# Row maxima, operand copies and value products of a prompt's attention, issued in another order

## The chip, the cores and the metric

The kernel runs on one core of a Trainium2 chip. The metric is the time on the device, in microseconds (us), of one launch; the lower the better. The core's engines each work through an instruction queue of their own, in order: TensorE (PE, whose weight loads show as PEld), VectorE (DVE), ScalarE (ACT), GpSimd (POOL), and SyncE (SP), which here only issues DMAs.

## The reference

One step of a two-layer model: layer 0 is a state-space mixer, layer 1 a latent attention with 16 heads. A prompt of 1024 tokens and 32 sample tokens go through both. The change lies in layer 1's attention of the prompt alone:

```python
def chunk_causal_attention(q_nope, q_rope, k_nope, k_rope, v, q_pos, k_pos):
    scale = MLA_QK ** -0.5                      # 64 + 32 columns per head
    k_chunk = k_pos // CHUNK                    # CHUNK = 64
    def block(args):
        qn, qr, qp = args
        s = (jnp.einsum('bqhd,bkhd->bhqk', qn, k_nope)
             + jnp.einsum('bqhd,bkd->bhqk', qr, k_rope)).astype(F32) * scale
        mask = k_chunk[None, :] <= (qp // CHUNK)[:, None]
        p = jax.nn.softmax(jnp.where(mask, s, -jnp.inf), axis=-1).astype(v.dtype)
        return jnp.einsum('bhqk,bkhd->bqhd', p, v)
```

All else (projections, norms, the gates, the mixer of layer 0, the output products) is the same in both kernels.

## The kernel before

Everything is computed in fp32, most products as three matmuls of a split operand: a rounded high part `h` and the rest `l = x - h`, summed as h*h + h*l + l*h. `phase_prompt` handles the 16 heads as 8 **pairs** `p`; a pair has two heads `par` = 0 and 1. Pairs alternate between two sets of operand buffers, `i = p % 2`; in the profile and in the orders below the tile of set `i` and head `par` is `qk` + `i` + `par` (`qk01`: set 0, head 1), with four parts `qh`, `kh`, `ql`, `kl`. 64 of the 128 rows of these tiles hold the head's own columns, and the others the rotary part and a few helper rows: a mask, and one row of `ql` that holds the negated row maxima of the scores, which the score product itself then subtracts.

So the steps of a pair are:

- `prep` (one or two pairs ahead): projections `psqk`, norm (`hn`), result in `hx`.
- `fill(p)`: copies of `hx` into `qh`/`kh` (rounded), the rest `hx - h` into `ql`/`kl` (by DVE for head 0, by POOL for head 1: `L_ENG`), and a DMA from POOL's queue for the rotary rows.
- `row_max(i, par)`: for each of 8 blocks of 128 queries one or two matmuls `s` into a PSUM tile (tag `s1`, two buffers, shared with `pm` and `sums`), each reduced by DVE into a column of `mx`; a last reduction (L1260); a transpose of `mx` by PE into `pm` (L1262); a negated copy by ACT into `mr` (L1264); and a DMA from POOL's queue (L1265) that writes `mr` into the row of `ql`.
- `pair(p)`: three **groups** of scores (`GROUPS`). Of each, 4 key blocks by 2 heads: three matmuls into `st` (two PSUM buffers), `exp` by ACT into `pf` (16 buffers). Behind the group stand its value products (`o`, 8 calls), and the sums over keys: additions of the `pf` tiles into `acc`, DVE for head 0 and POOL for head 1 (L1312 to L1318, one `acc` buffer for each head). `rest`, put behind the products of the next group, multiplies `acc` by ones (`sums`), takes the reciprocal as exp(-ln) and scales `o` (L1331).

While pair `p` is computed, `fill(p + 1)`, the row maxima of pair `p + 1` and `prep(p + 2)` run beside it. `spread` sets their order in the program: each stream has a number of steps, a step `k` of `n` stands at (k + 0.5) / n of the pair, and steps are sorted by it. A scheduler then moves instructions on each queue by its own estimate of times; what it made of both programs is shown with the change. Value projections (`psv`) of the next two pairs are put behind the second pair of two.

Of the kernel before, what the change touches and what calls it, by code (L numbers as in the profile page):

```python
# [10 lines left out]
F32 = mybir.dt.float32  # L11
F32R = mybir.dt.float32r
AF = mybir.ActivationFunctionType
ALU = mybir.AluOpType
# [3 lines left out]
P = 128  # L18
# [1097 lines left out]
L_ENG = ("vector", "gpsimd")  # L1116
# [56 lines left out]
def run(*gens):  # L1173
    for g in gens:
        for _ in g:
            pass


LEAD = 0.05


def spread(*streams):

    order = sorted(((k + 0.5) / n - lead, i) for i, (_, n, lead) in enumerate(streams) for k in range(n))
    for _, i in order:
        next(streams[i][0], None)
    run(*(g for g, _, _ in streams))


def phase_prompt(c, st, pr, before):  # L1190
    nc, tc, I, O = c.nc, c.tc, c.I, c.O
    es = ExitStack()
    ap_ = es.enter_context(tc.tile_pool(name="att", bufs=1, reuse_waits="tile"))
    before()
    aq = es.enter_context(tc.tile_pool(name="att2", bufs=1, reuse_waits="tile"))
    krt = ap_.tile([P, 1024], F32, tag="op", name="krt")
    nc.sync.dma_start(krt, c.kr_d[:, :1024])
    bufs = []
# [14 lines left out]
    def fill(p):  # L1213

        i, x = p % 2, pr.x.pop(p)
        qk = bufs[i]
        for par in range(2):
            r, rw = parts(par), rope_rows(par, i)
            eng = L_ENG[par]
            eng = getattr(nc, eng)  # L1220
            for a in range(4):
                dst = qk[("qh", "kh")[a // 2]][par][r, 512 * (a % 2) : 512 * (a % 2) + 512]
                nc.scalar.activation(dst, x[a][r], AF.Copy)
            nc.gpsimd.dma_start(qk["t"][par][rw, 0::2], pr.rope[rw])
            for a in range(4):
                cols = slice(512 * (a % 2), 512 * (a % 2) + 512)
                h, l = qk[("qh", "kh")[a // 2]][par][r, cols], qk[("ql", "kl")[a // 2]][par][r, cols]
                eng.tensor_tensor(l, x[a][r], h.bitcast(F32), op=ALU.subtract)  # L1228

    def values(g):  # L1230
        out = []
# [11 lines left out]
            out.append(vf)  # L1243
        return out

    def row_max(i, par):
        qk = bufs[i]
        qh, ql, kh, kl = (qk[n][par] for n in ("qh", "ql", "kh", "kl"))
        mrow = gap_rows(par, i).start + 10
        mx = ap_.tile([P, 16], F32, tag="mx", name="mx", bufs=2)  # L1250
        for b in range(8):
            n = max(256, 128 * (b + 1))
            ng, w = (1, n) if n <= 512 else (2, n // 2)
            for a in range(ng):
                ps = c.ps.tile([P, 512], F32, tag="s1", name="s1", bufs=2)
                nc.tensor.matmul(ps[:, :w], qh[:, 128 * b : 128 * b + 128], kh[:, a * w : a * w + w], start=True, stop=True)  # L1256
                col = b if b < 4 else 2 * b + a
                nc.vector.tensor_reduce(mx[:, col : col + 1], ps[:, : (w if b else 128)], axis=AX.X, op=ALU.max)  # L1258
            yield
        nc.vector.tensor_reduce(mx[:, 4:8], mx[:, 8:16].rearrange("p (a b) -> p a b", b=2), axis=AX.X, op=ALU.max)  # L1260
        pm = c.ps.tile([P, 512], F32, tag="s1", name="pm", bufs=2)
        nc.tensor.transpose(pm[:8, :128], mx[:, 0:8], c.ident)  # L1262
        mr = ap_.tile([8, 128], F32R, tag="mr", name="mr", bufs=2)
        nc.scalar.activation(mr, pm[:8, :128], AF.Copy, scale=-1.0)  # L1264
        nc.gpsimd.dma_start(ql[mrow : mrow + 1, :], mr)  # L1265

    def pair(p, vt, out):

        i = p % 2
        qk = bufs[i]  # L1270
        for g, (half, pieces) in enumerate(GROUPS):
            pfs = {}
            for j, q0, n in reversed(pieces):
                ks, q = slice(128 * j, 128 * j + 128), slice(q0, q0 + n)
                lo = max(q0, 128 * j) - q0
                for par in range(2):
                    qh, ql, kh, kl = (qk[nm][par] for nm in ("qh", "ql", "kh", "kl"))
                    ps = c.ps.tile([P, 512], F32, tag="st", name="st", bufs=2)
                    for t, (a_, b_) in enumerate(((kh, qh), (kh, ql), (kl, qh))):
                        nc.tensor.matmul(ps[:, :n], a_[:, ks], b_[:, q], start=t == 0, stop=t == 2)  # L1280
                    pf = aq.tile([P, 512], F32, tag="pf", name="pf", bufs=16)
                    nc.scalar.activation(pf[:, lo:n], ps[:, lo:n], AF.Exp, scale=SCALE)
                    f = q0 + lo - 512 * half
                    pfs[j, par] = pf[:, lo:n], slice(f, f + n - lo)
                    yield
            if g < 2:
                po = c.ps.tile([P, 512], F32, tag="o", name="o", bufs=2)

            def product(j, par):
                x, cols = pfs[j, par]  # L1290
                return nc.tensor.matmul(po[parts(par), cols], vt[j][:, i, par], x, start=j == 0,  # L1291
                                        stop=j == 4 * half + 3, skip_group_check=True)

            js = [j for j, _, _ in pieces]
            one = product(js[0], 1)
            with tc.issue_after(one.ins):
                product(js[0], 0)
                for j in js[1:]:
                    for par in range(2):
                        product(j, par)  # L1300
                if left:
                    left.pop()()

            if g < 2:
                acc = [aq.tile([P, 512], F32, tag=f"acc{par}", name="acc") for par in range(2)]
            for par in range(2):
                eng = (nc.vector, nc.gpsimd)[par]
                for k, j in enumerate(js):
                    x, cols = pfs[j, par]
                    a = acc[par][:, cols]  # L1310
                    if g == 2 or k > 1:
                        eng.tensor_tensor(a, a, x, op=ALU.add)  # L1312
                    elif k == 1:
                        f = cols.start
                        x0 = pfs[js[0], par][0]
                        if f:
                            eng.tensor_copy(acc[par][:, :f], x0[:, :f])
                        eng.tensor_tensor(a, x0[:, f:], x, op=ALU.add)  # L1318
            if g != 1:
                def rest(half=half, po=po, acc=acc):  # L1320
                    if half == 0:
                        out["o"] = ap_.tile([P, 1024], F32, tag="op", name="op")
                        out["sg"] = aq.tile([P, 1024], F32, tag="sg", name="sg")
                        nc.sync.dma_start(out["sg"], c.sg_d[p][:, :1024])
                    ps = c.ps.tile([P, 512], F32, tag="s1", name="sums", bufs=2)
                    for par in range(2):
                        nc.tensor.matmul(ps[parts(par)], c.ones[:, :64], acc[par], start=True, stop=True, skip_group_check=True)  # L1327
                    rec = acc[0]
                    nc.scalar.activation(rec, ps, AF.Ln)
                    nc.scalar.activation(rec, rec, AF.Exp, scale=-1.0)  # L1330
                    nc.vector.tensor_tensor(out["o"][:, 512 * half : 512 * half + 512], po, rec, op=ALU.mult)  # L1331
                left.append(rest)

    left = []
    pr.tag = "mm"

    operands(0)
    fill(0)
    run(row_max(0, 0))
    operands(1)  # L1340
    vt = values(0)
    run(row_max(0, 1))
    run(pr.prep(1))
    for p in range(8):
        g, i = p // 2, p % 2
        out = {}
        streams = [(pair(p, vt, out), 24, 0.0)]
        if p < 7:
            fill(p + 1)
            streams.append((itertools.chain(row_max(1 - i, 0), row_max(1 - i, 1)), 16, LEAD))  # L1350
        if p < 6:
            streams.append((itertools.chain(pr.prep(p + 2), pr.rope_block(g + 1) if i == 0 else ()), 6 if i == 0 else 4, LEAD))
# [195 lines left out]
```

## Time and profile before

| | us |
|---|---|
| median of 3 runs | 2036.13 (2035.63 to 2038.16) |
| the profiled execution, its time | 2041.28 |
| the profiled execution, its span (first to last instruction) | 2039.5 |
| of the span: PE busy | 1940.1 (95%) |
| DVE, ACT, POOL busy | 1185.4, 1011.9, 945.5 |
| prompt attention: first `s` matmul to last value product | about 1402 to 1838 |

The profiled execution was 5.2 us longer than the median run. A row of the profile gives the line of the code (a helper's line where a helper records the instruction), the engine, the operation, the tiles as out<-in, the shapes and the count; behind the bar stand busy time, the mean of one instruction in ns, and the engine's idle time just before these instructions with what ended it.

### The profile page before, as it was taken

Reading aid. Unit: us, or ns where it says so; the run is one execution under the profiler, and the core shown is the slowest. Engines: PE = TensorE matmul, PEld = TensorE weight load, DVE = VectorE, ACT = ScalarE, POOL = GpSimd, SP = SyncE. Lnnn points to the kernel's source line nnn. Section 1 sums busy time; section 2 is a strip of 40 time slices with the busy share of each in tenths; the row PEclk is TensorE's granted clock in tenths of the full one; section 3 lists DMA queues with packets and bytes.
Section 4 is the critical chain, followed back from the end, with each engine's and each line's share of the span. In section 5 each row is a group of like instructions: output and inputs, shape, how many; then the busy total and the mean of one; then the engine's idle time right before and its main releaser. Section 6 shows DMA issues by size and latency. Waiting matters only on the chain. (4 is left out here: it accounts for less than half of the span.)

```text
span 2039.5 us, 32319 instructions
## 1 busy us (share of the span) xinstructions
PE 1940.1 (95%) x12787; PEld 1733.4 (85%) x12787; DVE 1185.4 (58%) x1478; ACT 1011.9 (50%) x1875; POOL 945.5 (46%) x771
## 2 busy tenths in 40 slices
PE   8999999999999999999998999998989998889999
PEld 6988899999999998989998999676656565548999
DVE  6888675655757565352475453545465656645544
ACT  4436645455554547242334332875756565543331
POOL 5543534244343454545785441224344443635772
PEclk8999999999999999999999999999989998899999
DMA  4134333424233438453242223436121212315432
GB/s 138 53 84 97 89 94 88 103 74 92 89 77 95 115 80 299 123 181 114 90 127 85 83 95 110 133 92 150 30 59 47 52 40 52 109 53 180 136 122 75
DMA packets 110728, 204.24 MB, mean 100 GB/s; under 512 B 18224, under 2 KB 60720, under 8 KB 110448
## 3 DMA queue, kind: packets, MB, share of 16 engines
q1 hardware_dynamic: 105472, 193.17, 32.3%
q0 software_dynamic: 2800, 6.91, 1.8%
q8 instruction: 100, 1.64, 0.3%
q10 hardware_dynamic: 2304, 2.10, 0.3%
q14 instruction: 52, 0.43, 0.1%
HBM read 156.81 MB, written 38.83 MB: 96 GB/s over the span
## 5 line engine op out<-in xcount | busy, mean ns | idle before, releaser
L205 POOL TENSOR_TENSOR wl<-wraw,wh 128x1024 fp32r<-128x1024 f32 (+2 forms) x185 | 373.1, 2018 | 460.8 <-ACT wh L204 426.2
L215 PE MATMUL mm<-hh,wl 128*128 128x384 f32 (+2 forms) x1152 | 378.0, 328 | 0.0
L215 PE MATMUL mm<-hh,wh 128*128 128x384 f32 (+2 forms) x1152 | 377.1, 328 | 0.8 <-ACT hh L308 0.8
L215 PE MATMUL mm<-hl,wh 128*128 128x384 f32 (+2 forms) x1152 | 375.8, 327 | 0.0
L215 PE MATMUL pso<-yhl,wh 128*128 128x264 f32 x1536 | 285.2, 287 | 3.9 <-DVE yhl L229 1.9
L204 ACT ACTIVATE wh<-wraw 128x1024 fp32r<-128x1024 f32 (+2 forms) x182 | 157.8, 867 | 263.4 <-PE pso L215 102.2
L215 PEld LDWEIGHTS pso<-yhl,wh 128*128 128x128 f32 x1536 | 241.3, 190 | 6.9 <-DVE yhl L229 2.9
L215 PE MATMUL pso<-yhl,wl 128*128 128x264 f32 x768 | 219.9, 287 | 3.0 <-POOL wl L205 3.0
L215 PEld LDWEIGHTS mm<-hh,wh 128*128 128x128 f32 (+1 forms) x1152 | 216.2, 188 | 5.4 <-issue 2.8
L215 PEld LDWEIGHTS mm<-hl,wh 128*128 128x128 f32 (+1 forms) x1152 | 216.6, 188 | 1.6 <-issue 0.7
L215 PEld LDWEIGHTS mm<-hh,wl 128*128 128x128 f32 (+1 forms) x1152 | 216.4, 188 | 1.8 <-issue 0.3
L215 PE MATMUL psi<-yhl,wh 128*128 128x264 f32 (+1 forms) x896 | 166.9, 287 | 3.9 <-ACT yhl L228 3.8
L463 DVE SCALAR_TENSOR_TENSOR cx<-raw,pv,cx 128x1060 f32<-128x1060 f32 x96 | 142.4, 1487 | 41.1 <-ACT cx L461 40.5
L526 ACT ACTIVATE ex<-ex,tokT 128x128 f32<-128x128 f32 (+1 forms) x288 | 87.0, 380 | 133.9 <-DMA ex<-acs_d 126.7
L1258 DVE TENSOR_REDUCE mx<-s 128x1 f32<-128x128 f32 (+2 forms) x192 | 101.7, 552 | 84.5 <-PE s L1256 82.8
L1280 PE MATMUL st<-qk 128*128 128x512 f32 (+2 forms) x576 | 142.9, 378 | 6.8 <-DMA qk<-mr 5.1
L215 PEld LDWEIGHTS pso<-yhl,wl 128*128 128x128 f32 x768 | 146.1, 190 | 3.5 <-POOL wl L205 3.4
L215 PE MATMUL pg<-hH,wl 128*128 128x264 f32 x512 | 145.9, 285 | 0.3 <-POOL wl L205 0.3
L215 PE MATMUL pg<-hH,wh 128*128 128x264 f32 x512 | 145.9, 285 | 0.0
L215 PE MATMUL pg<-hL,wh 128*128 128x264 f32 x512 | 145.7, 285 | 0.0
L215 PEld LDWEIGHTS psi<-yhl,wh 128*128 128x128 f32 (+1 forms) x896 | 138.1, 185 | 5.6 <-ACT yhl L228 4.0
L1280 PEld LDWEIGHTS st<-qk 128*128 128x128 f32 x576 | 105.5, 206 | 35.5 <-issue 9.6
(517 smaller groups left out, 4289.6 us busy)
## 6 DMA issues: line engine op xcount, KB each, us to landing
wraw<-in_inW SPq DMA_DIRECT2D x48, 512.0 KB, 3.5
ex<-acs_d SPq DMA_DIRECT2D x32, 512.0 KB, 5.4
wraw<-in_outW SPq DMA_DIRECT2D x32, 512.0 KB, 3.7
yraw<-y_d SPq DMA_DIRECT2D x32, 264.0 KB, 5.0
u<-u_d SPq DMA_DIRECT2D x32, 264.0 KB, 2.8
eb<-ea_d SPq DMA_DIRECT2D x64, 128.0 KB, 3.9
y_d<-y SPq DMA_DIRECT2D x16, 512.0 KB, 2.9
wraw<-in_gateW SPq DMA_DIRECT2D x16, 512.0 KB, 3.6
```

The lines of the kernel that those rows point to most:

```text
L204: nc.scalar.activation(wh, raw, AF.Copy)
L205: nc.gpsimd.tensor_tensor(wl, raw, wh.bitcast(F32), op=ALU.subtract)
L215: c.nc.tensor.matmul(ps, ww[:, k, :m], aa, start=first and k == 0 and i == 0, stop=last and k == n - 1 and i == 2)
L463: nc.vector.scalar_tensor_tensor(xh, raw[:, k : k + T1], pvc(c, "cw", 4 * b + k), xh, op0=ALU.mult, op1=ALU.add)
L526: nc.scalar.activation(e_, e_, AF.Relu, scale=-1.0, bias=tok(32)[:, i, h : h + 1])
L1258: nc.vector.tensor_reduce(mx[:, col : col + 1], ps[:, : (w if b else 128)], axis=AX.X, op=ALU.max)
L1280: nc.tensor.matmul(ps[:, :n], a_[:, ks], b_[:, q], start=t == 0, stop=t == 2)
```

## The change

Five things are done, all in the prompt's attention:

1. `row_max` no longer ends with the transpose. The transpose, the copy and the DMA (`max_row`) stand behind later scores: those of head 0 behind three steps of head 1's maxima, those of head 1 behind two empty steps.
2. `spread` takes a start and an end for each stream. The maxima run from 0.2 to 0.9 of a pair with 18 steps (before: 16 steps from -0.05 to 0.95), and `fill` becomes a stream of 8 steps from 0 to 0.2 (before: all of it ahead of the pair).
3. In `fill` the rounded copies of head 0 go from ACT to DVE (`tensor_copy`, shown as CAST); those of head 1 stay on ACT. Each copy stands next to its subtraction.
4. The value products, the `acc` additions and the `rest` of a group are issued two key blocks (4 scores) into the next group; those of the last group at the end of the pair as before.
5. The pair's first maxima, ahead of the loop, follow the same scheme.

No matmul, exp, reduction or byte is added or removed; 32 copies change the engine.

```diff
 def spread(*streams):
-    order = sorted(((k + 0.5) / n - lead, i) for i, (_, n, lead) in enumerate(streams) for k in range(n))
+    order = sorted((a + (b - a) * (k + 0.5) / n, i) for i, (_, n, a, b) in enumerate(streams) for k in range(n))
...
     def fill(p):
...
-            for a in range(4):
-                dst = qk[("qh", "kh")[a // 2]][par][r, 512 * (a % 2) : 512 * (a % 2) + 512]
-                nc.scalar.activation(dst, x[a][r], AF.Copy)
             nc.gpsimd.dma_start(qk["t"][par][rw, 0::2], pr.rope[rw])
             for a in range(4):
...
-                eng.tensor_tensor(l, x[a][r], h.bitcast(F32), op=ALU.subtract)
+                if par:
+                    nc.scalar.activation(h, x[a][r], AF.Copy)
+                else:
+                    nc.vector.tensor_copy(h, x[a][r])
+                getattr(nc, L_ENG[par]).tensor_tensor(l, x[a][r], h.bitcast(F32), op=ALU.subtract)
+                yield
...
+    def max_row(i, par, mx):
+        mrow = gap_rows(par, i).start + 10
         pm = c.ps.tile([P, 512], F32, tag="s1", name="pm", bufs=2)
         nc.tensor.transpose(pm[:8, :128], mx[:, 0:8], c.ident)
         mr = ap_.tile([8, 128], F32R, tag="mr", name="mr", bufs=2)
         nc.scalar.activation(mr, pm[:8, :128], AF.Copy, scale=-1.0)
-        nc.gpsimd.dma_start(ql[mrow : mrow + 1, :], mr)
+        nc.gpsimd.dma_start(bufs[i]["ql"][par][mrow : mrow + 1, :], mr)
+
+    def row_maxima(i):
+        mx = [ap_.tile([P, 16], F32, tag="mx", name="mx", bufs=2) for _ in range(2)]
+        yield from row_max(i, 0, mx[0])
+        for k, _ in enumerate(row_max(i, 1, mx[1])):
+            if k == 2:
+                max_row(i, 0, mx[0])
+            yield
+        yield
+        yield
+        max_row(i, 1, mx[1])
...
     def pair(p, vt, out):
...
-            for j, q0, n in reversed(pieces):
+            for k, (j, q0, n) in enumerate(reversed(pieces)):
+                if k == 2 and late:
+                    late.pop()()
...
+            late.append(lambda *a, f=(g, half, [j for j, _, _ in pieces], pfs, po): group(p, vt, out, *f))
+        late.pop()()
...
-        streams = [(pair(p, vt, out), 24, 0.0)]
+        streams = [(pair(p, vt, out), 24, 0.0, 1.0)]
         if p < 7:
-            fill(p + 1)
-            streams.append((itertools.chain(row_max(1 - i, 0), row_max(1 - i, 1)), 16, LEAD))
+            streams.append((fill(p + 1), 8, 0.0, 0.2))
+            streams.append((row_maxima(1 - i), 18, 0.2, 0.9))
```

`group` holds what stood at the end of a group in `pair` before: products, additions, `rest`.

**What the scheduler made of it.** First PE's queue in the middle of pair 1, where the maxima of pair 2's head 0 end. `s` of `qk_14547` are the maxima scores of head 0, `s` of `qk_14548` those of head 1; `st` are pair 1's own scores (x3 is one tile), `pm` the transpose. Before:

```order
L1256 MATMUL s_15480<-qk_14547 128x512
L1280 MATMUL st<-qk_14617 128x512 x3
L1280 MATMUL st<-qk_14616 128x512 x3
L1262 MATMUL pm<-cst,mx 8x128
L1256 MATMUL s_15502<-qk_14548 128x256
L1280 MATMUL st<-qk_14617 128x512 x3
```

And now:

```order
L1251 MATMUL s_15467<-qk_14547 128x512
L1345 MATMUL sums<-acc,ones 64x512 x2
L1293 MATMUL st<-qk_14611 128x512 x3
L1293 MATMUL st<-qk_14612 128x512 x3
L1251 MATMUL s_15503<-qk_14548 128x256
L1251 MATMUL s_15512<-qk_14548 128x256
L1293 MATMUL st<-qk_14611 128x256 x3
L1251 MATMUL s_15521<-qk_14548 128x384
L1293 MATMUL st<-qk_14612 128x256 x3
L1308 MATMUL o<-pf,vf 64x512 x8
L1261 MATMUL pm<-cst,mx 8x128
```

Between the last score of head 0's maxima and the transpose stood two score tiles; now four, the sums, three scores of head 1's maxima and the eight value products.

Second, DVE's queue at the end of pair 1, where the maxima of head 1 end. `mx_15501` (before) and `mx_15370` (after) hold them; the row without `s1` is the last reduction, for which the transpose waits. Before:

```order
L1258 TENSOR_REDUCE mx_15501<-s1_15658 128x1
L1312 TENSOR_TENSOR acc_15579<-acc_15579,pf_15644 128x384
L1312 TENSOR_TENSOR acc_15579<-acc_15579,pf_15609 128x256
L1312 TENSOR_TENSOR acc_15579<-acc_15579,pf_15591 128x128
L1258 TENSOR_REDUCE mx_15501<-s1_15661 128x1
L1260 TENSOR_REDUCE mx_15501<-mx_15501 128x4
```

And now:

```order
L1223 CAST qk10_14611<-hx_15649 64x512
L1223 CAST qk10_14611<-hx_15424 64x512
L1224 TENSOR_TENSOR qk10_14611<-hx_15649,qk10_14611 64x512
L1224 TENSOR_TENSOR qk10_14611<-hx_15424,qk10_14611 64x512
L1253 TENSOR_REDUCE mx_15370<-s1_15577 128x1
L1253 TENSOR_REDUCE mx_15370<-s1_15586 128x1
L1253 TENSOR_REDUCE mx_15370<-s1_15589 128x1
L1253 TENSOR_REDUCE mx_15370<-s1_15598 128x1
L1253 TENSOR_REDUCE mx_15370<-s1_15601 128x1
L1255 TENSOR_REDUCE mx_15370<-mx_15370 128x4
L1349 TENSOR_TENSOR op_15619<-o_15401,acc_15486 128x512
L1334 TENSOR_TENSOR acc_15628<-pf_15519,pf_15500 128x512
```

The three additions that stood ahead of the last maxima have gone behind the last reduction; two of the new casts stand five reductions ahead of it, with their subtractions.

More of the change, by code (lines that the diff above doesn't have):

```diff
@@ L1176, in run @@
             pass
-LEAD = 0.05
 def spread(*streams):
-    order = sorted(((k + 0.5) / n - lead, i) for i, (_, n, lead) in enumerate(streams) for k in range(n))
+    order = sorted((a + (b - a) * (k + 0.5) / n, i) for i, (_, n, a, b) in enumerate(streams) for k in range(n))
     for _, i in order:
         next(streams[i][0], None)
-    run(*(g for g, _, _ in streams))
+    run(*(x[0] for x in streams))
 def phase_prompt(c, st, pr, before):
@@ L1244, in values, with row_max @@
         return out
[L1246 to L1250, printed above, removed]
+    def row_max(i, par, mx):
+        qh, kh = (bufs[i][n][par] for n in ("qh", "kh"))
         for b in range(8):
@@ L1287, in pair @@
                 po = c.ps.tile([P, 512], F32, tag="o", name="o", bufs=2)
-            def product(j, par):
-                x, cols = pfs[j, par]
[L1291 to L1302, printed above, removed]
@@ L1304, in pair @@
-            if g < 2:
-                acc = [aq.tile([P, 512], F32, tag=f"acc{par}", name="acc") for par in range(2)]
-            for par in range(2):
[L1307 to L1332, printed above, removed]
+            late.append(lambda *a, f=(g, half, [j for j, _, _ in pieces], pfs, po): group(p, vt, out, *f))
@@ new lines, in pair, with group, product, rest @@
+        late.pop()()
+    def group(p, vt, out, g, half, js, pfs, po):
+        def product(j, par):
+            x, cols = pfs[j, par]
+            return nc.tensor.matmul(po[parts(par), cols], vt[j][:, p % 2, par], x, start=j == 0,
+                                    stop=j == 4 * half + 3, skip_group_check=True)
+        one = product(js[0], 1)
+        with tc.issue_after(one.ins):
+            product(js[0], 0)
+            for j in js[1:]:
+                for par in range(2):
+                    product(j, par)
+            if left:
+                left.pop()()
+        if g < 2:
+            accs[:] = [aq.tile([P, 512], F32, tag=f"acc{par}", name="acc") for par in range(2)]
+        acc = list(accs)
+        for par in range(2):
+            eng = (nc.vector, nc.gpsimd)[par]
+            for k, j in enumerate(js):
+                x, cols = pfs[j, par]
+                a = acc[par][:, cols]
+                if g == 2 or k > 1:
+                    eng.tensor_tensor(a, a, x, op=ALU.add)
+                elif k == 1:
+                    f = cols.start
+                    x0 = pfs[js[0], par][0]
+                    if f:
+                        eng.tensor_copy(acc[par][:, :f], x0[:, :f])
+                    eng.tensor_tensor(a, x0[:, f:], x, op=ALU.add)
+        if g == 1:
+            return
+        def rest():
+            if half == 0:
+                out["o"] = ap_.tile([P, 1024], F32, tag="op", name="op")
+                out["sg"] = aq.tile([P, 1024], F32, tag="sg", name="sg")
+                nc.sync.dma_start(out["sg"], c.sg_d[p][:, :1024])
+            ps = c.ps.tile([P, 512], F32, tag="s1", name="sums", bufs=2)
+            for par in range(2):
+                nc.tensor.matmul(ps[parts(par)], c.ones[:, :64], acc[par], start=True, stop=True, skip_group_check=True)
+            rec = acc[0]
+            nc.scalar.activation(rec, ps, AF.Ln)
+            nc.scalar.activation(rec, rec, AF.Exp, scale=-1.0)
+            nc.vector.tensor_tensor(out["o"][:, 512 * half : 512 * half + 512], po, rec, op=ALU.mult)
+        left.append(rest)
@@ L1334, in phase_prompt @@
+    late, accs = [], []
     left = []
@@ L1337, in phase_prompt @@
     operands(0)
-    fill(0)
-    run(row_max(0, 0))
+    run(fill(0))
+    ahead = row_maxima(0)
+    for _ in range(8):
+        next(ahead)
     operands(1)
     vt = values(0)
-    run(row_max(0, 1))
+    run(ahead)
     run(pr.prep(1))
@@ L1346, in phase_prompt @@
         out = {}
-        streams = [(pair(p, vt, out), 24, 0.0)]
+        streams = [(pair(p, vt, out), 24, 0.0, 1.0)]
         if p < 7:
-            fill(p + 1)
-            streams.append((itertools.chain(row_max(1 - i, 0), row_max(1 - i, 1)), 16, LEAD))
+            streams.append((fill(p + 1), 8, 0.0, 0.2))
+            streams.append((row_maxima(1 - i), 18, 0.2, 0.9))
         if p < 6:
-            streams.append((itertools.chain(pr.prep(p + 2), pr.rope_block(g + 1) if i == 0 else ()), 6 if i == 0 else 4, LEAD))
+            streams.append((itertools.chain(pr.prep(p + 2), pr.rope_block(g + 1) if i == 0 else ()), 6 if i == 0 else 4, 0.0, 1.0))
         spread(*streams)
```

2 lines of the change are left out of this document (removed).

## The prediction

> **What bounds the kernel now.** I read the page first, for the engine that is full; then the prompt attention's stretch by windows, since the change touches nothing else; then who PE waits for there; then one such wait in order of time.
>
> ```profile
> span 2039.5 us, 32319 instructions
> PE 1940.1 (95%) x12787; PEld 1733.4 (85%) x12787; DVE 1185.4 (58%) x1478; ACT 1011.9 (50%) x1875; POOL 945.5 (46%) x771
> ```
>
> PE is the bound of the whole. The windows give, for each stretch, the busy time of PE, PEld, DVE, ACT and POOL, then the granted PE clock (PEclk), the DMA share and GB/s:
>
> ```profile
> 1402.00:1846.00 444.00, 392.12 (x1805) 261.18 (x1806) 262.87 (x409) 254.03 (x504) 195.03 (x184) 0.94 0.22 59
> 1500.00:1548.00 48.00, 39.79 (x202) 26.90 (x199) 30.78 (x49) 22.14 (x48) 25.19 (x25) 0.89 0.12 34
> 1548.00:1602.00 54.00, 50.48 (x216) 32.87 (x214) 31.44 (x46) 37.97 (x74) 20.25 (x19) 1.00 0.24 66
> 1602.00:1655.00 53.00, 47.03 (x242) 32.11 (x241) 35.55 (x58) 27.78 (x58) 28.49 (x28) 0.94 0.18 44
> 1846.00:2039.00 193.00, 188.96 (x1535) 188.49 (x1534) 95.80 (x92) 61.58 (x86) 112.60 (x60) 1.00 0.43 135
> ```
>
> The first row is the stretch at stake: PE idles 444.0 - 392.1 = 51.9 us, and its clock averages 0.94, so up to 0.06 x 444 = 26.6 us more are lost to slow matmuls. What follows (last row) runs at 98% and full clock. The rows between are single pairs: where PE idles much (8.2 of 48 us) the clock is 0.89, where little (3.5 of 54) it is 1.00. Idling is paid twice. Who PE waits for in that stretch (sum in us, times, longest):
>
> ```profile
> PE pm L1262 <- DVE mx L1260: 18.6, 10, 3.5
> PE s L1256 <- DVE mx L1258: 12.8, 23, 2.0
> PE o L1291 <- ACT pf L1282: 5.4, 11, 0.9
> PE st L1280 <- DMA qk<-mr: 5.1, 2, 2.9
> PE sums L1327 <- DVE acc L1312: 2.9, 1, 2.9
> ```
>
> The largest is the transpose of the maxima, waiting for DVE's last reduction. The rest of the 51.9 us are small waits and gaps without a named cause. One such wait, at the end of pair 0, in order of time (start, duration, engine, line; the last two rows are DVE's last reduction and PE's transpose, with PE's wait in brackets):
>
> ```profile
> 1500.55 0.52 PE L1280 MATMUL st<-qk 128*128 128x256 f32 x3
> 1500.26 3.44 DVE L1312 TENSOR_TENSOR acc<-acc,pf 128x384 f32<-128x384 f32 x3
> 1503.61 0.68 DVE L1258 TENSOR_REDUCE mx<-s 128x1 f32<-128x512 f32 x1
> 1504.33 0.16 DVE L1260 TENSOR_REDUCE mx<-mx 128x4 f32<-128x8 f32 x1
> 1504.54 0.37 PE L1262 MATMUL pm<-cst,mx 128*8 128x128 f32 x1 [3.47 <-DVE mx L1260]
> ```
>
> PE's scores were done at 1501.1. DVE spent 3.44 us on three `acc` additions that nobody was waiting for, and only then did the two reductions (0.84 us). PE's queue is in order, so everything behind the transpose stood still too. DVE isn't short of time: over the stretch it is busy 262.9 of 444 us.
>
> **The change, part by part.**
>
> *Transposes later, additions later (parts 1, 2, 4).* Behind head 0's last `s`, PE now has the sums, four score tiles, three `s` and the eight products before the transpose. Their prices, from another pair:
>
> ```profile
> 1743.81 3.65 PE L1291 MATMUL o<-pf,vf 128*64 128x512 f32 x16
> 1748.31 1.08 PE L1327 MATMUL sums<-acc,ones 128*64 128x512 f32 x4
> 1755.22 0.86 PE L1280 MATMUL st<-qk 128*128 128x512 f32 x3
> ```
>
> 3.65 + 1.08 + two tiles at 0.86 are 6.5 us, and DVE needs 0.84 us of reductions behind the last `s`; even with the 3.44 us of additions ahead of them that is covered. At head 1's end PE's work between last `s` and transpose stays about what it was, but in DVE's queue the three additions have gone behind the reduction: 0.84 us against the sums (1.08) and nine projection matmuls. So these waits should go. I keep one mean wait (18.6 / 10 = 1.9 us) for the step from pair 6 to pair 7, where DVE's new order still mixes seven additions and three splits of the next phase into the maxima, and little else is left to fill PE: **-16.7 us**. Ends: all of it (-18.6), or half (-9.3).
>
> *Copies to DVE (part 3).* Of the 56 copies in the stretch, half move:
>
> ```profile
> L1223 ACT ACTIVATE qk<-hx 64x512 fp32r<-64x512 f32 x56 | 35.0, 625 | 3.0 <-PE st L1280 2.3
> L202 DVE CAST wh<-wraw 128x1024 fp32r<-128x1024 f32 x2 | 1.4, 680 | 0.0
> L1317 DVE COPY acc<-pf x8: 217/852/1542, 1458.3 to 1820.7; 128x128 f32<-128x128 f32 x8
> L1317 POOL COPY acc<-pf x8: 289/290/292, 1462.1 to 1818.8; 128x128 f32<-128x128 f32 x8
> L1258 DVE TENSOR_REDUCE mx<-s 128x1 f32<-128x128 f32 (+2 forms) x192 | 101.7, 552 | 84.5 <-PE s L1256 82.8
> ```
>
> ACT gets back 28 x 0.625 = 17.5 us; it isn't what PE waits for, so I count nothing. The trace has no 64x512 cast on DVE. The nearest row is the 1024-column cast (0.68 us), half of it for 512 columns: 0.34 us alone. But the small COPY on DVE (minimum, median and maximum in ns) ranges from 217 to 1542 while the same copy on POOL stays at 290: DVE copies are held up when POOL works. I take 0.6 us: 28 x 0.6 = 16.8 us more for DVE, which has 181 us idle, 82.8 of them waiting for PE's own `s` (last row). PE pays only where a reduction that it waits for stands behind a cast; I take one in six, +2.8. In turn the additions that stood between reductions are gone from many places; of the 12.8 us of `s` waits I let as much go, -2.8. Together **0**; ends -6.4 (half the `s` waits) and +16.8 (every cast paid by PE).
>
> *Value products two key blocks later (part 4).* `o` won't wait for the exp just ahead of it in groups 0 and 1; at a pair's end nothing changes. Of 5.4 us **-1.5**; ends 0 and -2.7 (half). What it holds longer: 8 + 4 of 16 `pf` buffers, so exps have no new wait; if the additions fell back by a whole group, exps and with them scores would stop.
>
> *Queues and ends.* The first pair's transpose now stands behind three `s` of head 1 and so behind two more reductions (0.55 each, last row above), while the scores that need its row stay where they were: the 5.1 us of waits for `mr` grow by **+1.0** (0 to +2.2). In POOL's queue the `mr` DMA stands among additions as before. SP's output store moves a few places past loads of weights whose wait is not on PE's list: 0. At the very end, `rest` of half 0 comes one score tile later (0.52 us for 256 columns, row at 1500.55), and the chain of additions behind it, for which the sums wait, by as much: **+0.4**.
>
> Idle time: -16.7 + 0 - 1.5 + 1.0 + 0.4 = **-16.8 us**.
>
> *The clock.* In proportion to the idle time that goes: 26.6 x 16.8 / 51.9 = **-8.6 us** (ends: 0, and the whole 26.6).
>
> The Trainium skill (TensorE: Matmul & The Clock Gate, section on HAM oscillation) has the clock fall only after PE idles for more than about 3.4 us. By that rule only waits like the two longest transposes cost clock, both go, and the result would be the rival "clock full" below. The trace doesn't agree: the pair of 1602 to 1655 has a clock of 0.94, and no `s` wait anywhere is longer than 2.0 us.
>
> *What comes back.* PE that no longer waits reaches the next `s` earlier, and there are two PSUM buffers for it; DVE then has 262.9 + 16.8 = 279.7 us of work in some 420, 67% against 59%. I give back **+5 us** (a fifth of 25.4; ends 0 and all).
>
> Sum: -16.8 - 8.6 + 5 = -20.4 us. The profiled execution took 2041.3 us (its span 2039.5 and 1.8 around it), so 2020.9 for it; it was 5.2 us above the median of 2036.1, and from the median I forecast 2015.7, say **2016 us**, own range 2005 to 2026.
>
> **Rivals.**
>
> *The clock stays full.* The idle stretches that are left are too short and too far apart to lower it. For: the pair of 1548 to 1602 idles 3.5 us and has 1.00. Against: the tail's 2.9 us and the wait for `mr` remain. -16.8 - 26.6 + 5 = -38.4: 1998 us. Chance 0.12.
>
> *The wait moves.* DVE is just as late, and PE stops at the next `s` instead. For: `s` waits already happen 23 times. Against: DVE's additions now stand behind the maxima. Half the transposes' gain (-9.3, with -0.1 from the small terms), 4.8 of clock, 5 given back: -9.2, 2027 us. Chance 0.14.
>
> *Nothing comes of it.* PE's waits keep their sum, because DVE and POOL hold each other up, or because the `mr` row, which needs ACT, POOL's issue and the DMA (5.1 us waited for it already, in two waits), lands too late for head 1's scores at each pair's start: 2036 us. Against: DVE's 181 us of idle time. Chance 0.08.
>
> *The casts block DVE (slower).* Each cast waits for the POOL instruction that runs, and the reductions behind it wait too. Place: the four instructions ahead of head 1's last five reductions. At the longest COPY's 1.54 us, all paid by PE, 28 x 1.54 = 43 us: -25.4 + 43 = +17.7, 2054 us. It decides from 25.4 / 28 = 0.9 us per cast paid by PE. For: the COPY's median of 852 against 290. Against: only casts that stand ahead of a reduction due at once count. Chance 0.10.
>
> The Trainium skill (SBUF — State Buffer, section on who interferes with whom) says that VectorE's copies and casts in a two-port mode and GpSimd shut each other out for a whole instruction; the spread of the COPY agrees, and that rule is this rival.
>
> **How the numbers follow.** Forecast 0.56, clock full 0.12, wait moves 0.14, nothing 0.08, casts block 0.10. I predict the likeliest. The range 1997 to 2033 takes in all but the casts, nothing (half of it lies outside), and the far ends of the forecast. A change under 0.2% (4 us) can't be told from none: faster 0.80 (forecast, clock, most of the moved wait), same 0.09, slower 0.11.
>
> **What would show it.** In the profile after: the row of `pm` waiting for `mx` falls from 18.6 to under 4 us; `s` waiting for `mx` stays between 6 and 16; the stretch's PE idle is near 35 us and its clock about 0.96; the CAST's mean is 0.4 to 0.9 us; an undone wait shows as `s` far above 13. If DVE's casts average over 1.2 us, or `st` waits for `mr` at every pair, I am wrong on the sign; if the clock reads 0.99 or more, on the size.

## The result, and the profile after

The changed kernel takes 2051.68 us (median of 4 runs, 2047.70 to 2052.19) against 2036.73 us for the one before: a ratio of 1.0069, 95% interval 1.0051 to 1.0086. It is **slower by 0.7%**, where 2016 us were forecast. The profiled execution has a span of 2050.4 us, 10.9 us more than the one before (which lay 5 us above its median).

The page's first lines, and the attention's stretch by windows, up to the same point of the program (11 us later now):

```profile
span 2050.4 us, 32332 instructions
PE 1943.6 (95%) x12787; PEld 1736.6 (85%) x12787; DVE 1214.5 (59%) x1510; ACT 996.6 (49%) x1843; POOL 953.6 (47%) x771
```

```profile
1402.00:1857.00 455.00, 394.90 (x1807) 264.49 (x1806) 288.89 (x439) 240.89 (x476) 202.42 (x188) 0.92 0.22 59
```

PE idles 455.0 - 394.9 = 60.1 us (before 51.9), its clock is 0.92 (before 0.94), and DVE has 288.9 us of work (before 262.9). Who PE waits for in this stretch, the rows that the prediction has prices for (sum, times, longest):

```profile
PE s L1251 <- DVE mx L1253: 40.7, 22, 5.5
PE st L1293 <- DMA qk<-mr: 4.9, 2, 3.1
PE sums L1345 <- DVE acc L1328: 3.0, 1, 3.0
PE o L1308 <- ACT pf L1295: 2.3, 5, 0.7
```

The transpose's row (`pm`, 18.6 us) is gone, as forecast, and `o` fell from 5.4 to 2.3. But the scores of the maxima, `s`, wait 40.7 us for DVE's reductions instead of 12.8. DVE's groups in the stretch (busy us, mean ns of one, then idle time ahead of them):

```profile
L1253 DVE TENSOR_REDUCE mx<-s 128x1 f32<-128x128 f32 (+2 forms) x192 | 101.7, 551 | 79.5 <-PE s L1251 78.7
L1328 DVE TENSOR_TENSOR acc<-acc,pf 128x256 f32<-128x256 f32 (+1 forms) x64 | 59.5, 930 | 1.4
L1224 DVE TENSOR_TENSOR qk<-hx,qk 64x512 fp32r<-64x512 f32 x28 | 25.4, 918 | 0.2
L1223 DVE CAST qk<-hx 64x512 fp32r<-64x512 f32 x28 | 16.6, 601 | 7.7 <-PE st L1293 7.3
L1349 DVE TENSOR_TENSOR op<-o,acc 128x512 f32<-128x512 f32 x16 | 11.0, 689 | 24.7 <-ACT acc L1348 18.5 <-POOL acc L1334 6.1
```

The rows of the additions and the subtractions before:

```profile
L1312 DVE TENSOR_TENSOR acc<-acc,pf 128x256 f32<-128x256 f32 (+1 forms) x64 | 53.2, 831 | 1.2
L1228 DVE TENSOR_TENSOR qk<-hx,qk 64x512 fp32r<-64x512 f32 x28 | 21.2, 756 | 14.5 <-ACT qk L1223 14.5
```

The reductions take what they took. The additions went from a mean of 831 to 930 ns, the subtractions from 756 to 918, and the casts are new. Among the additions it is the widest that were stretched, the 24 of 128x512 (before, then now):

```profile
L1312 DVE TENSOR_TENSOR acc<-acc,pf 128x512 f32<-128x512 f32 x24 | 22.6, 941 | 0.5
L1328 DVE TENSOR_TENSOR acc<-acc,pf 128x512 f32<-128x512 f32 x24 | 36.3, 1512 | 0.7
```

The longest wait, at the start of pair 1, where the maxima of pair 2 begin, in order of time (DVE, then POOL, then PE):

```profile
1496.25 1.98 DVE L1223 CAST qk<-hx 64x512 fp32r<-64x512 f32 x1 [0.41 <-PE st L1293]
1498.16 0.68 DVE L1334 TENSOR_TENSOR acc<-pf 128x512 f32<-128x512 f32 x1
1498.76 0.48 DVE L1223 CAST qk<-hx 64x512 fp32r<-64x512 f32 x1
1499.16 1.75 DVE L1224 TENSOR_TENSOR qk<-hx,qk 64x512 fp32r<-64x512 f32 x1
1500.84 1.77 DVE L875 SCALAR_TENSOR_TENSOR hx<-hx,pv,hr__15655 128x512 f32<-128x512 f32 x1
1502.54 1.75 DVE L1328 TENSOR_TENSOR acc<-acc,pf 128x512 f32<-128x512 f32 x1
1504.22 1.47 DVE L1224 TENSOR_TENSOR qk<-hx,qk 64x512 fp32r<-64x512 f32 x1
1505.61 2.66 DVE L1328 TENSOR_TENSOR acc<-acc,pf 128x512 f32<-128x512 f32 x3
1508.19 0.61 DVE L1253 TENSOR_REDUCE mx<-s 128x1 f32<-128x128 f32 x2
```

```profile
1500.44 1.62 POOL L1328 TENSOR_TENSOR acc<-acc,pf 128x512 f32<-128x512 f32 x1
1502.14 1.60 POOL L1224 TENSOR_TENSOR qk<-hx,qk 64x512 fp32r<-64x512 f32 x1
1503.82 3.31 POOL L1328 TENSOR_TENSOR acc<-acc,pf 128x384 f32<-128x384 f32 x3
```

```profile
1501.53 0.40 PE L1251 MATMUL s<-qk 128*128 128x256 f32 x2
1501.77 1.26 PE L1293 MATMUL st<-qk 128*128 128x256 f32 x6
1508.53 1.12 PE L1251 MATMUL s<-qk 128*128 128x384 f32 x2 [5.50 <-DVE mx L1253]
```

PE had two scores of the next maxima done by 1502, filling both PSUM buffers, and stood from 1503.0 to 1508.5. DVE reached their reductions only at 1508.2: ahead of them stood a clump of casts, subtractions, one `hx` and additions. And four of these, from 1499.2 to 1505.7, took 1.5 to 1.8 us each, beside POOL's, two of which took 1.6 us; elsewhere in the traces the same shapes take about 0.7.

Two theories came out of this. **Queue**: what stood behind the old maxima now stands ahead of the new ones, and its number and length are the wait. **Contention**: DVE's instructions on SBUF tiles are stretched beside POOL's, and the new order brings the two together. A third was on record, the casts.

### The profile page after: what moved, and what is told of

The parts are those of the page before. It is cut to its first block, busy times and chain, and to the rows that moved or that the text cites. A ratio compares the mean times of both kernels' runs of the same rounds, so it can differ in the third digit from the quotient of the medians.

```text
span 2050.4 us, 32332 instructions
## 1 busy us (share of the span) xinstructions
PE 1943.6 (95%) x12787; PEld 1736.6 (85%) x12787; DVE 1214.5 (59%) x1510; ACT 996.6 (49%) x1843; POOL 953.6 (47%) x771
## 5 line engine op out<-in xcount | busy, mean ns | idle before, releaser
L1253 DVE TENSOR_REDUCE mx<-s 128x1 f32<-128x128 f32 (+2 forms) x192 | 101.7, 551 | 79.5 <-PE s L1251 78.7
L1295 ACT ACTIVATE pf<-st 128x128 f32<-128x128 f32 (+2 forms) x192 | 91.0, 490 | 99.4 <-PE st L1293 92.4
```

## Experiments

All ratios are to the kernel before, run on the same chip beside the kernel; in brackets is the 95% interval. The kernel before took 2036.7 to 2038.9 us (medians) in the five sets of runs, so times of different sets compare to about 2 us. A scheduler orders each kernel's queues anew, so an edit's price holds what that moves, too.

**One part undone at a time** (four kernels). The copies of head 0 back on ACT:

```diff
-                if par:
-                    nc.scalar.activation(h, x[a][r], AF.Copy)
-                else:
-                    nc.vector.tensor_copy(h, x[a][r])
+                nc.scalar.activation(h, x[a][r], AF.Copy)
```

> The changed kernel with part 3 undone: head 0's rounded copies are ACT's again. Theory (the clump: everything that stood behind the maxima now stands in DVE's queue ahead of the next ones, and PE stops at the third score): the 28 casts (16.6 us of DVE's time in the changed kernel) leave the clump, but additions, op product and subtractions stay, so waits of s for mx fall only from 40.7 us to 28 to 36 and the time to 2041 to 2049 us, still above before. Rival (the casts are what blocks DVE): waits of s fall to about the 12.8 us of before, and the time to 2025 us or less. Second rival (the casts cost nothing): s waits 38 to 42 us and 2050 to 2053 us.

2037.01 us, 0.9993 [0.9982, 1.0004]: the whole loss is gone, against 2051.68. `s` waits 30.9 us, as the theory had it, but the time is below its range: 28 casts cost some 15 us, 0.54 us each, which is nearly their whole busy time. How they cost it is not shown, though: over the whole run DVE's busy time falls by only 5.3 us with them (1214.5 to 1209.2), since subtractions (986 ns for 918) and first additions (1525 for 1308) are stretched more, and in the changed kernel DVE also stood 7.3 us ahead of the casts until PE's `st` was done. So not DVE's total work but what stands ahead of the reductions seems to be paid. And the waits stay far from the 12.8 us of before: the casts are not all of it.

The groups' products and additions back behind their own scores:

```diff
-                if k == 2 and late:
-                    late.pop()()
...
             late.append(lambda *a, f=(g, half, [j for j, _, _ in pieces], pfs, po): group(p, vt, out, *f))
-        late.pop()()
+            late.pop()()
```

> The changed kernel with part 4 undone: products, acc additions and rest stand at the end of their own group again. Theory (the clump): the additions go back between the scores of their own group and leave the head of the next maxima; waits of s for mx fall from 40.7 to 20 to 28 us, and the time to 2030 to 2042 us: the largest step of the four. Rival (casts block): s waits stay at 36 to 41 us and the time is 2048 to 2053 us. Another rival (what PE waits for at the products comes back: o and pm waits): s falls, but o and pm together rise by as much, 2048 to 2053 us.

2059.73 us, 1.0105 [1.0088, 1.0122]: slower still. The first theory is refuted in this form. `s` does fall to 18.2, but the transposes wait again, and `pm` and `o` (2.3 to 6.1) together rise by 21.4 us for the 22.5 that `s` loses. That is what the last rival said of the waits; the time is 7 us above all three cases:

```profile
PE s L1251 <- DVE mx L1253: 18.2, 24, 3.0
PE pm L1261 <- DVE mx L1255: 17.6, 7, 8.7
PE hn L872 <- ACT hsq L863: 9.0, 15, 1.2
```

Half of the `pm` row is one wait of 8.7 us, at the end of pair 5. There three splits of the next phase (`yhl`, 3.7 us for two and 2.2 us for one, beside POOL's splits of 2.8 us) stand in DVE's queue ahead of the last reduction.

The old windows, and `fill` ahead of the pair:

```diff
-            streams.append((fill(p + 1), 8, 0.0, 0.2))
-            streams.append((row_maxima(1 - i), 18, 0.2, 0.9))
+            run(fill(p + 1))
+            streams.append((row_maxima(1 - i), 18, -0.05, 0.95))
```

> The changed kernel with part 2 undone: the fill stands ahead of the pair, and the maxima run from -0.05 to 0.95 of it. Theory (the clump): scores of the maxima are spaced as before (18 steps over a whole pair instead of 0.7 of one), DVE has more time for each; but casts, subtractions and additions still stand in a clump ahead of the first reductions: s waits 26 to 36 us, 2038 to 2048 us. Rival (the spacing alone is the cause): s waits about 13 us, 2025 us or less. Rival (casts block): no change, 2049 to 2054 us.

2044.01 us, 1.0028 [1.0017, 1.0039], `s` waits 31.4 us: within the theory's numbers; the windows cost some 8 us.

The transposes back behind their own maxima:

```diff
-        for k, _ in enumerate(row_max(i, 1, mx[1])):
-            if k == 2:
-                max_row(i, 0, mx[0])
-            yield
-        yield
-        yield
+        max_row(i, 0, mx[0])
+        yield from row_max(i, 1, mx[1])
         max_row(i, 1, mx[1])
...
-            streams.append((row_maxima(1 - i), 18, 0.2, 0.9))
+            streams.append((row_maxima(1 - i), 16, 0.2, 0.9))
```

> The changed kernel with part 1 undone: each transpose stands immediately behind its maxima. Theory: PE then waits at the transposes (pm) as it did before, some 10 to 18 us, and what stands behind is late by as much, so part of the s waits turns into pm waits: s 28 to 36 us, pm 10 to 18 us, the time 2050 to 2060 us, so the late transposes by themselves were a gain of 0 to 8 us. Rival (the late transposes are what moved the wait): s falls by as much as pm rises and the time is unchanged, 2050 to 2053 us. If the time falls below 2045 us, the late transposes did harm of their own, which neither says.

2070.93 us, 1.0161 [1.0142, 1.0181]: the worst of all. `s` waits 30.6 and `pm` 21.1 us. Late transposes save some 19 us in this order, more than any of the theories had.

**Some parts alone.** Parts 1 and 4 (copies and windows taken back as in the first and the third edit above):

> Parts 1 and 4 alone: late transposes and deferred groups, with the copies on ACT and the windows of before. If the costs of casts (14.7 us, from the run without them) and of the windows (7.7 us) are separate and add up, 2051.7 - 14.7 - 7.7 = 2029 us (2026 to 2033), faster than before, with waits of s for mx of some 20 us. If both work through the same clump in DVE's queue, most of the gain is already had by taking out one, and the time is 2034 to 2038 us with s waits of 28 us or more.

2037.27 us, 1.0000 [0.9988, 1.0012], `s` waits 29.0 us: the second case. Casts and windows do not add up. And part 1 alone (the second edit on top):

> Part 1 alone: late transposes, all else as before. By the steps of the prediction this is the step worth -16.7 us, so 2015 to 2028 us with pm waits under 4 us and s waits near the 12.8 us of before. By the theory of the moved wait: DVE's additions stand among the maxima as before, so what PE no longer waits for at the transpose it waits for at a later score: pm under 4, s waits 22 to 30 us, 2030 to 2037 us. If the deferral of the groups is worth its 8 us also here: 2037 us.

2037.70 us, 0.9993 [0.9983, 1.0003]: nothing. What PE no longer waits for at the transpose is waited for elsewhere:

```profile
PE s L1248 <- DVE mx L1250: 17.3, 23, 3.5
PE st L1288 <- DMA qk<-mr: 7.8, 3, 3.2
PE o L1303 <- ACT pf L1290: 7.5, 13, 1.2
PE pm L1258 <- DVE mx L1250: 4.5, 4, 1.4
PE hn L872 <- ACT hsq L863: 4.5, 8, 1.2
PE pm L1258 <- DVE mx L1252: 1.4, 4, 0.5
```

`pm` lost 12.7 us (18.6 less 4.5 and 1.4); `s`, `mr`, `o` and `hn` (2.4 before) took 4.5 + 2.7 + 2.1 + 2.1 = 11.4 of them. `s` rose less than the theory said.

**POOL or the queue.** The changed kernel without POOL's additions, so that the sums of head 1 are missing:

```diff
-            accs[:] = [aq.tile([P, 512], F32, tag=f"acc{par}", name="acc") for par in range(2)]
+            accs[:] = [aq.tile([P, 512], F32, tag="acc0", name="acc")] * 2
...
-        for par in range(2):
+        for par in (0,):
             eng = (nc.vector, nc.gpsimd)[par]
```

> The changed kernel without POOL's additions: the sums of head 1 are left out, and head 1's output is scaled by head 0's sums. This takes away what POOL does beside DVE's work (some 13 additions and copies a pair), and none of DVE's own. If POOL's reads and writes stretch DVE's instructions (contention): DVE's acc addition falls from a mean of 930 ns to under 720, the cast from 601 to under 450, the subtraction from 918 to under 720, and the waits of s for mx from 40.7 to under 22 us; 2020 to 2038 us. If the sheer number of instructions ahead of the reductions is the cause (queue): the durations fall little or the waits stay above 30 us, 2043 us or more.

2010.78 us, 0.9867 [0.9853, 0.9880]: 41 us below the changed kernel, though DVE has as many instructions as there (1510 in the whole run).

```profile
PE s L1251 <- DVE mx L1253: 13.5, 18, 2.9
```

```profile
L1328 DVE TENSOR_TENSOR acc<-acc,pf 128x256 f32<-128x256 f32 (+1 forms) x64 | 40.6, 634 | 1.3
L1223 DVE CAST qk<-hx 64x512 fp32r<-64x512 f32 x28 | 13.0, 472 | 5.2 <-PE st L1293 4.7
L1349 DVE TENSOR_TENSOR op<-o,acc 128x512 f32<-128x512 f32 x16 | 11.0, 688 | 27.4 <-ACT acc L1348 27.4
```

Additions of 930 ns take 634. The multiplication `op`, which reads one operand from PSUM, takes 688 as ever (689 beside POOL). The casts (472) and the subtractions (872) fell less than expected, but POOL's own subtractions still run. The counterpart, with DVE's additions, and so the sums of head 0, left out (`par in (1,)` and `acc1`):

> The changed kernel without DVE's additions: the sums of head 0 are left out, and head 0's output is scaled by head 1's sums. DVE loses 88 instructions and some 85 us; POOL keeps its own. Queue: the clump ahead of the maxima loses most of its length, s waits fall from 40.7 to under 14 us, 2015 to 2030 us. Contention, with the casts and subtractions as what is stretched: casts stay near 600 ns, subtractions near 900, s waits 20 to 32 us, 2033 to 2045 us.

2009.83 us, 0.9863 [0.9850, 0.9875], `s` waits 9.1 us, casts 692 ns, subtractions 820: what the queue expected, and faster. Either side taken away brings the same 41 us, so this pair alone does not tell number from stretching. Moving the work does:

```diff
-            eng = (nc.vector, nc.gpsimd)[par]
+            eng = nc.vector
```

> The changed kernel with all acc additions on DVE, head 1's too; nothing is left out. Contention: DVE's additions take about the 634 ns that they took without POOL's, but there are twice as many, some 65 us more in the same queue, ahead of the maxima: s waits 35 to 55 us and 2045 to 2070 us. If stretched instructions alone were the cause, and not also their number, s waits fall to 14 to 25 us and the time to 2015 to 2035 us.

2025.66 us, 0.9934 [0.9918, 0.9951]: 26 us faster than the changed kernel and faster than the one before. **Contention** has the larger part: DVE has 88 additions and copies more in the same places, and PE waits less.

```profile
PE s L1251 <- DVE mx L1253: 12.9, 14, 2.5
```

```profile
PE 1939.7 (96%) x12787; PEld 1731.0 (85%) x12787; DVE 1223.7 (60%) x1598; ACT 995.7 (49%) x1843; POOL 860.0 (42%) x683
```

```profile
L1328 DVE TENSOR_TENSOR acc<-acc,pf 128x512 f32<-128x512 f32 (+3 forms) x128 | 69.9, 568 | 1.1
```

Twice the additions (128 for 64, in the same mix of shapes) cost DVE 69.9 us instead of 59.5. With each sum's first addition and copy it is 112.2 us instead of 85.5, 26.7 more; yet over the whole run DVE is busy only 9.2 us more (1223.7 against 1214.5), so its other work took some 17 us less. One thing is not separated: without POOL's additions DVE no longer stands ahead of `op` for them, 6.1 us in the changed kernel (row L1349 above). The same edit with `nc.gpsimd`:

> The changed kernel with all acc additions on POOL, head 0's too; nothing is left out. By the shown costs DVE loses 85 us and its queue ahead of the maxima the additions: s waits fall from 40.7 to 8 to 16 us. POOL has some 85 to 100 us more, 300 of 458. If POOL's lateness stays hidden: 2010 to 2022 us, faster than both kernels. Rival (POOL becomes late: the sums wait for its additions at each pair, and the mr rows queue behind them): sums and st waits of 20 us or more, 2035 us or slower.

2049.17 us, 1.0048 [1.0032, 1.0064]. Slow, but not in the rival's way: the sums wait 8.4 us for POOL, once, and `st` 3.7 for `mr`; the bulk is `s` again, 34.7 us, with one wait of 13.8 us, though DVE has much less work (235.4 us from 1402 to 1860, against 288.9). The place is shown at the end.

**The old order under the same edits.** The kernel before without POOL's additions, then with all of them on POOL, then with all of them on DVE:

> The kernel before, without POOL's additions: the sums of head 1 are left out, and head 1's output is scaled by head 0's sums (the same cut that brought the changed kernel to 2010.8 us). If the order of the change is a gain that DVE and POOL's holding each other up took away: the old order keeps its pm waits (10 to 16 us), and the time is 2022 to 2032 us, slower than the changed order under the same cut by more than 10 us. If the order is worth nothing even then: 2008 to 2015 us, the same as 2010.8 within 5. If the old order didn't suffer from POOL at all: 2033 us or more.

2018.26 us, 0.9903 [0.9886, 0.9920]; `pm` waits 9.0 us. The changed order under the same edit (0.9867) is faster by 0.36%, 7 us: between the first two cases. The old order loses 20 us to POOL's additions, the new one 41.

> The kernel before with all acc additions on POOL; nothing is left out. The 3.44 us of additions ahead of the last maxima leave DVE's queue: pm waits fall from 18.6 to 8 to 14 us (0.84 us of reductions stay ahead of each transpose), s waits from 12.8 to under 10; 2015 to 2030 us. If the changed order is then worth its gain, the changed kernel with the same edit is faster than this by 5 us or more. Rival (POOL late): sums waits, 2035 us or slower.

2032.04 us, 0.9971 [0.9958, 0.9984]: `pm` 1.0 us, but `mr` 10.6 and the sums 7.8; a little slower than expected, a little faster than before. With the same edit the changed order (2049.17) is 17 us slower than this, not 5 us faster: with all additions on POOL the order is a loss as well.

> The kernel before with all acc additions on DVE, head 1's too; nothing is left out. With POOL out of the additions the new order gives 2025.7 us. If the loss of the change comes from the new order meeting POOL, the new order is a gain here: the old one keeps twice the additions ahead of its last maxima, pm waits 12 to 22 us, 2029 to 2040 us, slower than 2025.7 by 3 us or more. If the order is worth nothing once POOL is quiet: 2022 to 2028 us. If it is a loss even then: under 2022 us.

2037.73 us, 0.9996 [0.9983, 1.0008]: nothing, as the first case says. `pm` still waits:

```profile
PE pm L1262 <- DVE mx L1260: 15.9, 10, 3.5
PE s L1256 <- DVE mx L1258: 8.1, 22, 1.0
```

So with POOL out of the additions and nothing left out, the new order is a gain of 12 us (0.9934 against 0.9996); with POOL in them a loss of 15.

**Casts and windows with POOL quiet.** All additions on DVE, and the copies back on ACT:

> The changed kernel with all acc additions on DVE and head 0's copies back on ACT; nothing is left out. Beside POOL's additions the casts on DVE cost 14.7 us. If they cost it because POOL stretches them and their neighbours, they are cheap here (a mean of 451 ns): 2019 to 2026 us. If they cost it because DVE's queue is long ahead of the maxima, and it is longer here: the gain is again 12 us or more, 2008 to 2014 us.

2015.95 us, 0.9886 [0.9863, 0.9908]: **the fastest that computes everything, 1.1% below the kernel before**. The casts cost 9.7 us here, between the two cases: about two thirds of their price (with an uncertainty of some 5 us) doesn't need POOL's additions. DVE's queue length counts as well. With the windows of before on top:

> Late transposes and deferred groups alone (copies on ACT, windows of before), with all acc additions on DVE; nothing is left out. With POOL's additions parts 2 and 3 cost 14.7 us together (2037.3 against 2051.9). If the windows cost nothing where DVE is not stretched: the same as the kernel with the casts taken back alone, within 4 us. If the spacing of the maxima matters by itself (7.7 us in the run with the old windows): 5 us or more faster than that one.

2022.21 us, 0.9913 [0.9894, 0.9932]. If anything slower by 6 us, against both cases, but the intervals overlap: what the windows do with POOL quiet stays open.

## Why the prediction was wrong, point by point

**Two steps failed.** The forecast was 20.4 us faster, and the kernel became 15 us slower. With the copies back on ACT, the rest of the change gains nothing (0.9993): that is some 20 of the 35 us between, and the step behind it is that the transposes' waits would go for -16.7 us, with +5 for what comes back. The other 15 us are the copies' "Together 0".

**The transposes' -16.7 us.** The `pm` row fell from 18.6 to nothing, and late transposes do save some 19 us within the new order. But the step from a wait that goes to time that goes was wrong. Alone, late transposes bring nothing (0.9993), and in the new order with the copies back on ACT the scores `s` wait 30.9 us instead of 12.8. The rival "the wait moves" is what the changed kernel's waits show: its "against", that DVE's additions now stand behind the maxima, overlooked that behind one pair's maxima is ahead of the next pair's.

What ate the gain is POOL's additions beside DVE's work. With all additions on DVE in both orders, and the copies on ACT, the new order gains 22 us (2015.95 against 2037.73, with an uncertainty of some 5 us). That this is close to the 20.4 forecast may be luck, as no term was measured there alone. The rival "nothing comes of it" had named the cause, that DVE and POOL hold each other up; I set it aside for DVE's idle time.

**The copies' "Together 0".** The price of a cast agreed (0.6 us taken, a mean of 601 ns measured), with some luck: the median is 419 ns, and the longest took 1981. The share that PE pays was wrong: I let it pay one cast in six, 2.8 us, and took the same off the `s` waits. Taking the casts back is worth some 15 us, near my bound of +16.8 for every cast paid, to which I gave less weight than to the 181 us of DVE's idle time. These lie elsewhere: DVE still waits 78.7 us for PE's `s` over the stretch, and is late in the few microseconds between two maxima.

**The price that was missing: the other instructions' stretching.** I costed the moved additions and subtractions at nothing, as if their durations came with them. The additions rose by 6.3 us (53.2 to 59.5) and the subtractions by 4.2 (21.2 to 25.4). With the casts' 16.6 that is 27.1, about all of DVE's 26.0 us more (262.9 to 288.9), where I had 16.8. The trace of before had shown it: the 128x512 additions averaged 941 ns, and the seven of the 24 that met no POOL instruction took 675 to 694.

The Trainium skill (SBUF — State Buffer, section on who interferes with whom), which I had cited for copies alone, also says that a VectorE instruction with two SBUF inputs contends with a GpSimd instruction that reads SBUF, and one with at most one SBUF input outside the two-port modes doesn't. Here the trace agrees: 930 ns against 634 for the additions without POOL's, 689 and 688 for the product with a PSUM operand, 551 for the reductions throughout.

**The casts' rival** had the time (2054, measured 2051.7), but not the way, so its near hit is luck: a cast takes 0.60 us on average, not 1.54, and its threshold of 0.9 us per cast doesn't hold, because the 25.4 us that it was to eat up never came.

**What comes back** (+5) was the right thought and too small: `s` rose by 27.9 us, more than the 25.4 I had as its end. **The clock** went the other way with the idle time, 0.94 to 0.92, somewhat more than by the proportion that I had used (0.08 x 455 = 36 us on 60 us of idling). **The products** (-1.5) were near: `o` fell by 3.1, but `st` waits for exps rose by 1.7. **`mr`** (+1.0): 4.9 us, no change. **The tail** (+0.4): 3.0 against 2.9 us. Of the marks I had set, `pm` under 4, and casts of 0.4 to 0.9 us, held; `s` between 6 and 16, idle near 35 and a clock of 0.96 did not. The two signs for being wrong on the sign (casts over 1.2 us, `st` waiting for `mr` at every pair) did not come, though the sign was wrong; the one for an undone wait, `s` far above 13, did.

## What to carry to other kernels

Taking away PE's largest wait may bring nothing if the engine it waited for is just as late at the next thing that PE asks of it: with an in-order queue and two PSUM buffers, look at what stands in that engine's queue ahead of the *next* request, not only of this one. DVE's idle time over a whole stage is no cover for work that is issued in the few microseconds where PE waits for it. And two engines that share a sum may be slower than one: where DVE's additions run beside POOL's, price them from rows where both run, and try all of them on DVE.

## What the hardware showed that I had not expected

DVE is not only slowed beside POOL; it can stand still behind a whole row of POOL's instructions. With all additions on POOL, one split of 128x528 elements (about 0.7 us alone) took 13.67 us, until POOL's row, 13.6 us without a gap, ended:

```profile
1758.79 13.67 DVE L229 TENSOR_TENSOR yhl<-yraw,yhl 128x528 fp32r<-128x528 f32 x1
1772.38 1.07 DVE L1253 TENSOR_REDUCE mx<-s 128x1 f32<-128x512 f32 x2
```

```profile
1758.29 1.29 POOL L1334 TENSOR_TENSOR acc<-pf 128x512 f32<-128x512 f32 x1
1759.53 4.92 POOL L1328 TENSOR_TENSOR acc<-acc,pf 128x512 f32<-128x512 f32 x4
1764.42 2.33 POOL L205 TENSOR_TENSOR wl<-wraw,wh 128x1024 fp32r<-128x1024 f32 x1
1766.71 0.98 POOL L1328 TENSOR_TENSOR acc<-acc,pf 128x384 f32<-128x384 f32 x1
1767.66 2.33 POOL L205 TENSOR_TENSOR wl<-wraw,wh 128x1024 fp32r<-128x1024 f32 x1
1769.96 1.93 POOL L1328 TENSOR_TENSOR acc<-acc,pf 128x512 f32<-128x512 f32 x2
```

PE waited 13.8 us for the reduction behind it. Two `hx` instructions of the same run took 6.64 us each (0.75 us alone); the first, from 1547.77, got its turn before POOL's row ended at 1555.9. Why POOL keeps its turn through a row here, while in the changed kernel the two took turns at 1.6 and 1.75 us, no run told.
